# Weights' roundings queued behind evacuations, an earlier first memset, another queue for one load, and a new last quarter

## The chip, the cores and the metric

One core of one Trainium2 chip runs the kernel. The metric is the device time of one execution in microseconds (us), as the median of the timed runs. A profile is one further execution, recorded by the hardware profiler. TensorE (PE) multiplies matrices, VectorE (DVE), ScalarE (ACT) and GpSimd (POOL) work on tiles, and SyncE (SP) mostly issues DMAs. Each engine takes its own instructions strictly in order; between engines semaphores decide.

## The reference

One layer of an encoder for 2 x 256 tokens of width 1024, all in float32, with three branches on one normalized input:

```
h = rmsnorm(x);  proj = h @ w_in          # qkv | decays | z | cq | ckv | z_mla | q_mem | z_mem | gates
A: conv + silu on qkv, gated delta rule in both directions, rmsnorm per head, * silu(z)
B: q = rmsnorm(cq) @ w_q_up (+ rope), k|v = rmsnorm(ckv) @ w_kv_up (+ rope), softmax(q k) v, * silu(z_mla)
C: 4-head attention into 256 memory tokens, k|v = rmsnorm(mem) @ w_mem_kv, * silu(z_mem)
y = rmsnorm(x + (sum over branches of sigmoid(gate) * (o @ w_br)) @ w_out)
```

## The kernel before, in words

**Split products.** Every float32 operand is split into a high part (rounded to TensorE's fp32r) and a low part (the rest), and a product is three passes: high x high, low x high, high x low. Names end in h and l for data (`hh`, `hl`, `klh`, `kll`, `qlh`, `vh`, `vl`), and begin with `wh_` and `wl_` for weights. `weight()` (L224) brings a weight: SP loads it raw (`wr_`, L229), ACT rounds it to `wh_` (L241), DVE subtracts to get `wl_` (L244). Each of the three kinds has two buffers, so that a load waits for the subtraction two weights back and a rounding for the matmuls two weights back. `gemm` (L264) runs 24 matmuls of 512 columns for a weight of 1024 rows, 9 or 6 for a shorter one. `split()` (L249) evacuates a product from PSUM in the same two steps: ACT rounds (L252), DVE subtracts (L254).

**Stages.** The front (up to about 346 us) makes the memory keys and values (`mem_v`), the latents, and branch B: `mla_v` makes the values of four heads at a time (`v03`, `v10` to `v13`, first digit the half, second the token block), `mla_qk` the keys (`kn4`: head 4) and queries (`qn4`), `attend` the softmax and the product with the values (`a71`: head 7, half 1; `p_`, its transpose `pt_`, split to `ph_` and `pl_`, product `oa`). The rotary queries (`ra`, `rb`, then `rt`, split to `rh` and `rl`) go to DRAM (`d_q`) and come back in another layout (`qs`) by DMAs on SP. Tiles of branch A's projection (`qkv11`, `qkv18`, with a convolution on ACT and DVE: `cz`, `kq`, `vf`), z tiles (`za`) and gates (`g02`) fill the gaps. The middle runs branch A, the back the merge and `output`, which makes the rows of y in token blocks 0 to 3: the left half of all four, then the right half of blocks 0 to 2, then block 3's right half in two quarters, `y20` and `y21`.

**What sets the order.** The code issues steps, and a scheduler of the tile framework puts each engine's instructions into an order, by its own estimate of when they can run, by priority (`high_priority(offset=...)` puts an instruction ahead of others) and by explicit constraints: `issue_after(i)` keeps an instruction behind instruction i in the order, and adds no wait. In the middle, steps of branch A are generators with due times: `yield a, b` hands back the cost of a step and the distance after which the next is due.

**The places that the change touches.** In `mem_v` a 128x512 tile of zeros (`zero`, L387) feeds ten warm-up matmuls (`zp`, L390); `prm`, the small parameters (gains, convolution weights; 87 KB), is the second load on SP's queue (L405), and ACT and DVE need it for `mh`, the scaled memory tokens (L419, L420). In `attend` six matmuls (L366) run in the order (vh, ph), (vh, pl), (vl, ph) for each of two key blocks. In `gdn_out` the sum of squares of a head's output is reduced on DVE (L1181, into `rr`) and comes to TensorE a step later (`so`, L1185). In `output` the last quarter adds the residual on DVE (L1393), squares and sums (L1394), takes the power on GpSimd (L1396), and scales and stores.

Of the kernel before, what the change touches and what calls it, by code (L numbers as in the profile page):

```python
# [181 lines left out]
class Layer:  # L182
    def __init__(self, tc, A):
        self.tc, self.nc, self.A, self.hold = tc, tc.nc, A, None


# [37 lines left out]
    def weight(self, src, n, name, pool=None, into=None):  # L224
# [14 lines left out]
        hi = place("wh_", "wh")  # L239
        with self.tc.high_priority(offset=60):  # L240
            self.wround = nc.scalar.activation(hi[:, :n], raw[:, :n], AF.Copy).ins  # L241
# [78 lines left out]
    def attend(self, h, s, score, scale, vs, op, name):  # L320
# [40 lines left out]
        self.plast = self.lsplit  # L361
        n = 0
        for kb in range(2):
            q = slice(kb * 256, (kb + 1) * 256)
            for a, b in ((vs[kb][0], hi), (vs[kb][0], lo), (vs[kb][1], hi)):
                nc.tensor.matmul(pairs(op), a, turns(b[:, q]), start=n == 0, stop=n == 5)  # L366
# [12 lines left out]
    def mem_v(self):  # L379
        nc, A = self.nc, self.A  # L380
        ms = []
        warm = self.p0.tile([P, 1], F32, name="warm")
# [4 lines left out]
        nc.vector.memset(zero.bitcast(F32), 0.0)  # L387
        zp = self.ps_kk("zp")
        for i in range(10):
            nc.tensor.matmul(zp, zero[:, 0:P], zero, start=i == 0, stop=i == 9)  # L390

# [3 lines left out]
        with self.tc.high_priority(offset=1000):  # L395
            for k in range(8):
# [7 lines left out]
                if k == 0:  # L404
                    nc.sync.dma_start(self.prm, A["prm"])  # L405
# [740 lines left out]
    def gdn_out(self, hh):  # L1146
# [32 lines left out]
        with self.behind():  # L1179
            nc.vector.transpose(out=st, in_=sq)  # L1180
            nc.vector.tensor_reduce(red, st.rearrange("p (j i) -> p j i", i=32), axis=AX.X, op=ALU.add)  # L1181
# [140 lines left out]
    def output(self):  # L1322
# [16 lines left out]

        def product(ps, hi, lo, j, tb, c0=0, c1=512):  # L1340
            t = slice(tb * P, (tb + 1) * P)
            n = 0
            for q in range(2):
                for a, b in ((0, hi), (1, hi), (0, lo)):
                    nc.tensor.matmul(pairs(ps), xs[2 * j + q][a][:, t],  # L1345
                                     turns(b[:, q * 512:(q + 1) * 512])[:, c0 // 2:c1 // 2],
                                     start=j == 0 and n == 0, stop=j == 3 and n == 5)
# [34 lines left out]

        s3, out = ss[3], A["ys"][0, P:2 * P]
        for q in range(2):
            ps = self.ps_kk(f"y2{q}")
            for j in range(4):
                product(ps[:, 0:256], *ws[j], j, 3, 256 * q, 256 * q + 256)
            if q == 0:
                y = add(ps[:, 0:256], 3, 2, 256)
                nc.vector.tensor_scalar(s3[:, 0:1], s3[:, 1:2], 1.0 / D, s3[:, 0:1], ALU.mult, ALU.add)  # L1390
                nc.gpsimd.tensor_tensor(y, y, fg[:, 512:768], op=ALU.mult)
        y = ys[3][:, 768:1024]
        nc.vector.tensor_tensor(y, y, ps[:, 0:256], op=ALU.add)  # L1393
        nc.vector.tensor_tensor_reduce(self.ct("jk")[:, 0:256], y, y, 1.0 / D, s3[:, 0:1], ALU.mult, ALU.add, s3[:, 2:3])  # L1394
# [1 line left out]
        nc.gpsimd.tensor_tensor(r, s3[:, 2:3], self.c("hf")[:, 0:1], op=ALU.pow)  # L1396
# [1 line left out]
        nc.scalar.activation(ys[3][:, 0:448], ys[3][:, 0:448], AF.Copy, scale=r)
        nc.scalar.dma_start(out[:, 0:448], ys[3][:, 0:448])
        nc.vector.tensor_scalar(ys[3][:, 448:1024], ys[3][:, 448:1024], r, None, ALU.mult)  # L1400
# [321 lines left out]
```

## Time and profile before

| | |
|---|---|
| median of 3 runs | 798.67 us (798.55 to 798.84) |
| the profiled execution's own time | 798.48 us |
| its span | 796.7 us |
| TensorE busy | 786.6 us (99%) |
| VectorE busy | 579.2 us (73%) |
| ScalarE busy | 447.4 us (56%) |
| GpSimd busy | 166.9 us (21%) |
| granted TensorE clock | 0.999 |

How to read the rows. A row of the timeline is: start in us from the span's start, duration, engine and line, operation, tile written <- tiles read (without buffer numbers), shape, how many in a row, and in brackets how long the engine had been idle and what ended that. SPq and ACTq are DMA issues by these engines. A row of the waits names the engine and line that waited, what released it, and total, number and longest wait. A row of the DMA issues ends with the size of one and the median time from issue to landing. A matmul's duration includes its way through the array, so matmuls in a row start closer together than they last. TensorE's busy share is that of its queue being full, not of its peak.

### The profile page before, as it was taken

Reading aid. Unit: us, or ns where it says so; the run is one execution under the profiler, and the core shown is the slowest. Engines: PE = TensorE matmul, PEld = TensorE weight load, DVE = VectorE, ACT = ScalarE, POOL = GpSimd, SP = SyncE. Lnnn points to the kernel's source line nnn. Section 1 sums busy time; section 2 is a strip of 40 time slices with the busy share of each in tenths; the row PEclk is TensorE's granted clock in tenths of the full one; section 3 lists DMA queues with packets and bytes.
Section 4 is the critical chain, followed back from the end, with each engine's and each line's share of the span. In section 5 each row is a group of like instructions: output and inputs, shape, how many; then the busy total and the mean of one; then the engine's idle time right before and its main releaser. Section 6 shows DMA issues by size and latency. Waiting matters only on the chain.

```text
span 796.7 us, 13067 instructions
## 1 busy us (share of the span) xinstructions
PE 786.6 (99%) x4774; PEld 692.9 (87%) x4774; DVE 579.2 (73%) x974; ACT 447.4 (56%) x894; POOL 166.9 (21%) x135
## 2 busy tenths in 40 slices
PE   9999999999999999999999999999999999999996
PEld 7888898889898899988888888888888888888886
DVE  7886358787699999669599989498565655465543
ACT  6755465556565565646757556667766463322332
POOL 0200111000010002154221226540512003333312
PEclk9999999999999999999999999999999999999999
DMA  9523222732417635444444435555653557464532
GB/s 325 177 78 102 93 77 81 229 124 70 116 61 211 192 96 141 142 133 154 129 155 133 146 120 160 172 151 175 192 172 119 172 181 256 160 197 153 178 107 105
DMA packets 68911, 118.18 MB, mean 148 GB/s; under 512 B 23664, under 2 KB 31344, under 8 KB 68848
## 3 DMA queue, kind: packets, MB, share of 16 engines
q1 hardware_dynamic: 67552, 115.03, 45.9%
q10 hardware_dynamic: 1296, 2.33, 0.8%
q8 instruction: 37, 0.61, 0.3%
q14 instruction: 26, 0.21, 0.1%
HBM read 98.24 MB, written 19.09 MB: 147 GB/s over the span
## 4 chain that ended last, share of the span: by engine, by line
PE 91%; DVE 4%; DMA 1%; ACT 1%; issue 1%; POOL 0%; SPq 0%; POOLq 0%; ACTq 0%; DVEq 0%
PE gm_qkv L276 14%; PE gm_g L276 14%; PE gm_z L276 7%; PE gm_za L276 5%; PE gm_bm L276 5%; PE y L1345 5%; PE vm L427 3%; PE gm_be L276 3%; PE gm_qm L276 3%; PE gm_km L276 3%; PE gm_bg L276 3%; PE o L1163 2%; PE gm_bg L1312 2%; PE s_a L330 2%; PE kk L1012 2%; PE gm_qn L276 2%
## 5 line engine op out<-in xcount | busy, mean ns | idle before, releaser
L776 DVE SCALAR_TENSOR_TENSOR kq<-cz,prm,kq 128x510 f32<-128x510 f32 (+1 forms) x64 | 52.0, 813 | 2.2 <-ACT kq L769 1.3
L276 PE MATMUL gm_qkv<-hl,wh_qkv 128*128 128x512 f32 x192 | 49.0, 385 | 0.0
L276 PE MATMUL gm_g<-hh,wl_g 128*128 128x512 f32 x192 | 48.8, 384 | 0.0
L276 PE MATMUL gm_g<-hh,wh_g 128*128 128x512 f32 x192 | 48.0, 385 | 0.0
L276 PE MATMUL gm_g<-hl,wh_g 128*128 128x512 f32 x192 | 47.2, 382 | 0.0
L276 PE MATMUL gm_qkv<-hh,wl_qkv 128*128 128x512 f32 x192 | 47.0, 382 | 0.0
L276 PE MATMUL gm_qkv<-hh,wh_qkv 128*128 128x512 f32 x192 | 46.8, 381 | 0.0
L1287 POOL TENSOR_TENSOR mg<-mg,lg 128x512 f32<-128x512 f32 x16 | 29.5, 1849 | 73.2 <-DVE lg L1286 31.8
L244 DVE TENSOR_TENSOR wl_g<-wr_g,wh_g 128x1024 fp32r<-128x1024 f32 x24 | 31.2, 1300 | 17.1 <-PE gm_g L276 9.3
L244 DVE TENSOR_TENSOR wl_qkv<-wr_qkv,wh_qkv 128x1024 fp32r<-128x1024 f32 x24 | 31.0, 1290 | 13.6 <-ACT wh_qkv L241 7.7
L1022 DVE SCALAR_TENSOR_TENSOR ne<-e,cc,kk 128x512 f32<-128x512 f32 (+1 forms) x64 | 35.7, 608 | 6.2 <-ACT ed L843 2.7
L276 PEld LDWEIGHTS gm_qkv<-hh,wh_qkv 128*128 128x128 f32 x192 | 35.8, 189 | 5.1 <-ACT wh_qkv L241 0.3
L276 PEld LDWEIGHTS gm_g<-hl,wh_g 128*128 128x128 f32 x192 | 35.9, 189 | 4.7
L276 PEld LDWEIGHTS gm_qkv<-hh,wl_qkv 128*128 128x128 f32 x192 | 35.8, 189 | 4.8
L276 PEld LDWEIGHTS gm_g<-hh,wh_g 128*128 128x128 f32 x192 | 35.4, 189 | 4.8
L276 PEld LDWEIGHTS gm_qkv<-hl,wh_qkv 128*128 128x128 f32 x192 | 35.4, 189 | 4.7
L276 PEld LDWEIGHTS gm_g<-hh,wl_g 128*128 128x128 f32 x192 | 35.4, 189 | 4.5
L969 POOL TENSOR_SCALAR_AFFINE_SELECT e<-e 128x256 f32<-128x256 f32 x32 | 20.0, 651 | 90.2 <-DMA e<-d_r 75.1
L1345 PE MATMUL y<-wh_wo,mh 128*128 128x512 f32 (+1 forms) x144 | 37.7, 356 | 0.0
L241 ACT ACTIVATE wh_g<-wr_g 128x1024 fp32r<-128x1024 f32 x24 | 25.3, 1052 | 19.9 <-PE gm_g L276 7.2
L1188 POOL TENSOR_TENSOR rr<-rr,cst 32x16 f32<-32x16 f32 x8 | 25.0, 3123 | 46.6 <-DVE rr L1187 46.4
L241 ACT ACTIVATE wh_qkv<-wr_qkv 128x1024 fp32r<-128x1024 f32 x24 | 25.3, 1055 | 15.1 <-DVE vf L776 3.2
(458 smaller groups left out, 2189.4 us busy)
## 6 DMA issues: line engine op xcount, KB each, us to landing
wr_g<-in_w_dram SPq DMA_DIRECT2D x24, 512.0 KB, 4.0
wr_qkv<-in_w_dram SPq DMA_DIRECT2D x24, 512.0 KB, 3.8
e<-d_r SPq DMA_DIRECT2D x64, 96.0 KB, 3.0
wr_z<-in_w_dram SPq DMA_DIRECT2D x12, 512.0 KB, 3.6
d_g<-gt_g SPq DMA_DIRECT2D x16, 256.0 KB, 2.5
wr_za<-in_w_dram SPq DMA_DIRECT2D x8, 512.0 KB, 3.6
lg<-d_g SPq DMA_DIRECT2D x16, 256.0 KB, 3.9
wr_bm<-in_w_dram SPq DMA_DIRECT2D x8, 512.0 KB, 3.8
```

The lines of the kernel that those rows point to most:

```text
L241: self.wround = nc.scalar.activation(hi[:, :n], raw[:, :n], AF.Copy).ins
L244: self.wsplit = nc.vector.tensor_tensor(lo[:, :n], raw[:, :n], hi[:, :n].bitcast(F32), op=ALU.subtract).ins
L276: nc.tensor.matmul(pairs(ps[:m]), a[:, k * m:(k + 1) * m], turns(xs[k][j]), start=n == 0, stop=n == 3 * nk - 1)
L330: nc.tensor.matmul(pairs(sp[:, qb * 256:(qb + 1) * 256]), a, turns(b), start=j == 0, stop=j == n - 1)
L427: nc.tensor.matmul(pairs(vps[tb]), ms[k][a][:, t], turns(b[:, :512]), start=k == 0 and i == 0, stop=k == 7 and i == 2)
L776: nc.vector.scalar_tensor_tensor(ys, zs, self.cw[:, f, m:m + 1], ys, ALU.mult, ALU.add)
L969: self.nc.gpsimd.affine_select(out=e[:, :, r], in_=e[:, :, r], pattern=[[0, 2], [sg, 128]], compare_op=ALU.is_ge, fill=NEG, base=0, channe ...
L1012: nc.tensor.matmul(pairs(ps), a[:, k], turns(b), start=i == 0, stop=i == 2)
L1022: nev = nc.vector.scalar_tensor_tensor(ne[:, :, d, s, r], es[d][:, s, r].unsqueeze(1).to_broadcast([P, 2, n]), cc[:, d, w:w + 1], kin, ALU ...
L1188: nc.gpsimd.tensor_tensor(rr, rr, c("hf")[last, 0:1].to_broadcast([32, 16]), op=ALU.pow)
L1287: nc.gpsimd.tensor_tensor(self.merged[d], self.merged[d], gt, op=ALU.add)
L1345: nc.tensor.matmul(pairs(ps), xs[2 * j + q][a][:, t], turns(b[:, q * 512:(q + 1) * 512])[:, c0 // 2:c1 // 2], start=j == 0 and n == 0, sto ...
```

## The change

Five edits:

1. `free(a)` is new: `mla_v` and `mla_qk` register their evacuations in a bank, and `weight()` keeps its rounding and its subtraction behind the evacuations that were registered before the previous weight. It is an order on the same engine, not a wait.
2. `attend` for `a71` runs the four matmuls with `ph` ahead of the two with `pl`.
3. `mem_v` writes a 128x128 tile of zeros first (its matmuls read it four times over), and `prm` is loaded from GpSimd's queue.
4. `gdn_out` lets head 5's `so` come 13 instead of 12 later, as head 7's.
5. `output` puts the residual of the last quarter into PSUM (a first matmul that only opens the accumulation, then a copy over it), squares and sums on ACT from PSUM, and gives 480 columns of the last scaling to ACT and 544 to DVE, the last 256 of these straight from PSUM.

```diff
     def __init__(self, tc, A):
+        self.bank = [[], []]
...
-        with self.tc.high_priority(offset=60):
+        with self.tc.high_priority(offset=60), ExitStack() as st:
+            for i in self.bank[0]:
+                st.enter_context(self.tc.issue_after(i))
+            self.bank = [self.bank[1], []]
             self.wround = nc.scalar.activation(hi[:, :n], raw[:, :n], AF.Copy).ins
...
+    def free(self, a):
+        self.bank[1] += [a.ins, self.lsplit]
...
-        n = 0
-        for kb in range(2):
-            q = slice(kb * 256, (kb + 1) * 256)
-            for a, b in ((vs[kb][0], hi), (vs[kb][0], lo), (vs[kb][1], hi)):
-                nc.tensor.matmul(pairs(op), a, turns(b[:, q]), start=n == 0, stop=n == 5)
-                n += 1
+        order = [(kb, i, b) for kb in range(2) for i, b in ((0, hi), (0, lo), (1, hi))]
+        if name == "a71":
+            order.sort(key=lambda o: o[2] is lo)
+        for n, (kb, i, b) in enumerate(order):
+            nc.tensor.matmul(pairs(op), vs[kb][i], turns(b[:, kb * 256:(kb + 1) * 256]), start=n == 0, stop=n == 5)
...
+        zero = self.s2("zero", F32R)[:, 0:P]
+        nc.vector.memset(zero.bitcast(F32), 0.0)
         warm = self.p0.tile([P, 1], F32, name="warm")
...
-            nc.tensor.matmul(zp, zero[:, 0:P], zero, start=i == 0, stop=i == 9)
+            nc.tensor.matmul(zp, zero, zero.unsqueeze(1).to_broadcast([P, 4, P]), start=i == 0, stop=i == 9)
...
-                    nc.sync.dma_start(self.prm, A["prm"])
+                    nc.gpsimd.dma_start(self.prm, A["prm"])
...
-            self.split(ps, vh, vl)
+            self.free(self.split(ps, vh, vl))
...
-            self.split(unpaired(ps), halves(hi), halves(lo))
+            self.free(self.split(unpaired(ps), halves(hi), halves(lo)))
...
-        yield 0.0, 13 if hh == 7 else 12
+        yield 0.0, 13 if hh in (5, 7) else 12
...
+        parts = [self.ps_kk(f"y2{q}")[:, 0:256] for q in range(2)]
+        product(parts[1], *ws[0], 0, 3, 256, 512, 1)
+        nc.vector.tensor_copy(parts[1], y)
...
-        nc.vector.tensor_tensor(y, y, ps[:, 0:256], op=ALU.add)
-        nc.vector.tensor_tensor_reduce(self.ct("jk")[:, 0:256], y, y, 1.0 / D, s3[:, 0:1], ALU.mult, ALU.add, s3[:, 2:3])
+        nc.scalar.activation(self.ct("jk")[:, 0:256], ps, AF.Square, accum_out=s3[:, 2:3])
+        nc.vector.tensor_scalar(s3[:, 2:3], s3[:, 2:3], 1.0 / D, s3[:, 0:1], ALU.mult, ALU.add)
...
-        nc.vector.tensor_tensor(y, y, fg[:, 768:1024], op=ALU.mult)
-        nc.scalar.activation(ys[3][:, 0:448], ys[3][:, 0:448], AF.Copy, scale=r)
-        nc.scalar.dma_start(out[:, 0:448], ys[3][:, 0:448])
-        nc.vector.tensor_scalar(ys[3][:, 448:1024], ys[3][:, 448:1024], r, None, ALU.mult)
-        nc.sync.dma_start(out[:, 448:1024], ys[3][:, 448:1024])
+        nc.scalar.activation(ys[3][:, 0:480], ys[3][:, 0:480], AF.Copy, scale=r)
+        nc.scalar.dma_start(out[:, 0:480], ys[3][:, 0:480])
+        nc.vector.scalar_tensor_tensor(y, ps, r, fg[:, 768:1024], ALU.mult, ALU.mult)
+        nc.vector.tensor_scalar(ys[3][:, 480:768], ys[3][:, 480:768], r, None, ALU.mult)
+        nc.sync.dma_start(out[:, 480:1024], ys[3][:, 480:1024])
```

What the first edit does to the order shows on the engines' own lists. The numbers behind a name count buffers; the lines of the changed kernel are 4 to 7 higher. First ACT around the rounding of `qkv11`'s weight, before and after:

```order
L769 ACTIVATE kq2_1653<-cz_10_1654,prm_76 128x2x256
L241 ACTIVATE wh_qkv11_1703<-wr_qkv11_1701 128x1024
L252 ACTIVATE vh03_1681<-v03_1674 128x512
L241 ACTIVATE wh_qn0_1744<-wr_qn0_1742 128x384
L252 ACTIVATE kn0_1698<-gm_kn0_1691 128x512
```

```order
L774 ACTIVATE kq2_1653<-cz_10_1654,prm_76 128x2x256
L256 ACTIVATE vh03_1681<-v03_1674 128x512
L245 ACTIVATE wh_qkv11_1703<-wr_qkv11_1701 128x1024
L256 ACTIVATE kn0_1698<-gm_kn0_1691 128x512
L245 ACTIVATE wh_qn0_1744<-wr_qn0_1742 128x384
```

The two evacuations, `vh03` and `kn0`, have each changed places with the rounding ahead of them. The second place is ACT from `rh11` (rotary queries) to the rounding of `qn4`'s weight, before and after:

```order
L252 ACTIVATE rh11_2687<-rt_2682 128x512
L241 ACTIVATE wh_kn4_2886<-wr_kn4_2884 128x256
L767 ACTIVATE cz_18_2849<-gm_qkv18_2823 128x512
L769 ACTIVATE vf2_2848<-cz_18_2849,prm_76 128x512
L777 ACTIVATE cz_2_2776<-kq2_1653 128x512
L241 ACTIVATE wh_g03_2916<-wr_g03_2914 128x1024
L252 ACTIVATE vh11_2813<-v11_2806 128x512
L241 ACTIVATE wh_qn4_2954<-wr_qn4_2952 128x384
L252 ACTIVATE vh12_2869<-v12_2862 128x512
L252 ACTIVATE kn4_2901<-gm_kn4_2890 128x512
L252 ACTIVATE vh13_2880<-v13_2873 128x512
```

```order
L772 ACTIVATE cz_18_2849<-gm_qkv18_2823 128x512
L256 ACTIVATE rh11_2687<-rt_2682 128x512
L774 ACTIVATE vf2_2848<-cz_18_2849,prm_76 128x512
L782 ACTIVATE cz_2_2776<-kq2_1653 128x512
L256 ACTIVATE vh11_2813<-v11_2806 128x512
L245 ACTIVATE wh_kn4_2886<-wr_kn4_2884 128x256
L256 ACTIVATE vh12_2869<-v12_2862 128x512
L256 ACTIVATE vh13_2880<-v13_2873 128x512
L245 ACTIVATE wh_g03_2916<-wr_g03_2914 128x1024
L256 ACTIVATE kn4_2901<-gm_kn4_2890 128x512
L245 ACTIVATE wh_qn4_2954<-wr_qn4_2952 128x384
```

All four evacuations of the values and the keys now stand ahead of `wh_qn4`, three of them ahead of `wh_g03`, and `rh11` has come behind `cz_18`. On TensorE the same stretch, from the last value matmuls to the first with `g03`'s weight, before and after:

```order
L717 MATMUL v11_2806<-wl_wv1_2793,klh1_1113 128x512
L276 MATMUL gm_kn4_2890<-klh0_1108,wh_kn4_2886 128x512
L276 MATMUL gm_kn4_2890<-klh1_1113,wh_kn4_2886 128x512
L276 MATMUL gm_kn4_2890<-kll0_1109,wh_kn4_2886 128x512
L276 MATMUL gm_kn4_2890<-kll1_1114,wh_kn4_2886 128x512
L276 MATMUL gm_kn4_2890<-klh0_1108,wl_kn4_2888 128x512
L276 MATMUL gm_kn4_2890<-klh1_1113,wl_kn4_2888 128x512
L276 MATMUL gm_g03_2920<-hh0_339,wh_g03_2916 128x512
```

```order
L722 MATMUL v13_2873<-wl_wv1_2793,klh1_1113 128x512
L283 MATMUL gm_kn4_2890<-klh0_1108,wh_kn4_2886 128x512
L283 MATMUL gm_kn4_2890<-klh1_1113,wh_kn4_2886 128x512
L283 MATMUL gm_kn4_2890<-kll0_1109,wh_kn4_2886 128x512
L283 MATMUL gm_kn4_2890<-kll1_1114,wh_kn4_2886 128x512
L283 MATMUL gm_g03_2920<-hh0_339,wh_g03_2916 128x512
```

`v13` is now the last of the values instead of `v11`, and four instead of six `kn4` matmuls lie between it and `g03`; `gm_qkv18`'s end, which stood ahead of `v12` to `v11` (18 matmuls), now stands ahead of two of `v12`'s, `v11` and `v13` (14). The third place is TensorE ahead of `g02`, before and after:

```order
L276 MATMUL ra1_2625<-qlh2_897,wl_ra1_2630 128x512
L356 MATMUL pt_a21_2446<-cst_311,p_a21_2438 128x128 x4
L366 MATMUL oa2_2384<-ph_a20_2413,vh00_1607 128x256
L366 MATMUL oa2_2384<-pl_a20_2414,vh00_1607 128x256
L366 MATMUL oa2_2384<-ph_a20_2413,vl00_1608 128x256
L366 MATMUL oa2_2384<-ph_a20_2413,vh01_1618 128x256
L366 MATMUL oa2_2384<-pl_a20_2414,vh01_1618 128x256
L366 MATMUL oa2_2384<-ph_a20_2413,vl01_1619 128x256
L356 MATMUL pt_a30_2570<-cst_311,p_a30_2562 128x128 x4
L276 MATMUL gm_g02_2713<-hh0_339,wh_g02_2709 128x512
```

```order
L283 MATMUL ra1_2625<-qlh0_823,wl_ra1_2630 128x512
L283 MATMUL ra1_2625<-qlh1_859,wl_ra1_2630 128x512
L283 MATMUL ra1_2625<-qlh2_897,wl_ra1_2630 128x512
L846 MATMUL dp01_2078<-dr01ct_2055,bd_1325 128x512
L283 MATMUL gm_g02_2713<-hh0_339,wh_g02_2709 128x512
```

Before, the transposes of `a21` and `a30` and the products of `a20` stood between `ra1` and `g02`; now there is one matmul, `dp01`, and the attention's come later.

More of the change, by code (lines that the diff above doesn't have):

```diff
@@ L384, in mem_v @@
         nc.scalar.activation(warm, warm, AF.Square)
-        zero = self.s2("zero", F32R)
-        nc.vector.memset(zero.bitcast(F32), 0.0)
-        zp = self.ps_kk("zp")
+        zp = self.ps_kk("zp").rearrange("p (a b) -> p a b", a=4)
         for i in range(10):
-            nc.tensor.matmul(zp, zero[:, 0:P], zero, start=i == 0, stop=i == 9)
+            nc.tensor.matmul(zp, zero, zero.unsqueeze(1).to_broadcast([P, 4, P]), start=i == 0, stop=i == 9)
         vps = [self.ps_gm(f"vm{tb}") if tb == 3 else self.ps_ms(tb % 2, f"vm{tb}") for tb in range(4)]
@@ L1338, in output, with product @@
             ss.append(self.pe.tile([P, 4], F32, name=f"yss{tb}"))
-        def product(ps, hi, lo, j, tb, c0=0, c1=512):
+        def product(ps, hi, lo, j, tb, c0=0, c1=512, last=24, seeded=False):
             t = slice(tb * P, (tb + 1) * P)
@@ L1344, in product @@
                 for a, b in ((0, hi), (1, hi), (0, lo)):
-                    nc.tensor.matmul(pairs(ps), xs[2 * j + q][a][:, t],
-                                     turns(b[:, q * 512:(q + 1) * 512])[:, c0 // 2:c1 // 2],
-                                     start=j == 0 and n == 0, stop=j == 3 and n == 5)
+                    if 6 * j + n < last:
+                        nc.tensor.matmul(pairs(ps), xs[2 * j + q][a][:, t],
+                                         turns(b[:, q * 512:(q + 1) * 512])[:, c0 // 2:c1 // 2],
+                                         start=j == 0 and n == 0 and not seeded, stop=j == 3 and n == 5)
                     n += 1
@@ L1381, in output @@
             nc.sync.dma_start(out[:, 512:1024], y)
-        s3, out = ss[3], A["ys"][0, P:2 * P]
-        for q in range(2):
-            ps = self.ps_kk(f"y2{q}")
+        s3, out, y = ss[3], A["ys"][0, P:2 * P], ys[3][:, 768:1024]
+        parts = [self.ps_kk(f"y2{q}")[:, 0:256] for q in range(2)]
+        product(parts[1], *ws[0], 0, 3, 256, 512, 1)
+        nc.vector.tensor_copy(parts[1], y)
+        for q, ps in enumerate(parts):
             for j in range(4):
-                product(ps[:, 0:256], *ws[j], j, 3, 256 * q, 256 * q + 256)
+                product(ps, *ws[j], j, 3, 256 * q, 256 * q + 256, 24, q == 1)
             if q == 0:
-                y = add(ps[:, 0:256], 3, 2, 256)
+                x = add(ps, 3, 2, 256)
                 nc.vector.tensor_scalar(s3[:, 0:1], s3[:, 1:2], 1.0 / D, s3[:, 0:1], ALU.mult, ALU.add)
[L1391 to L1394, printed above, removed]
+                nc.gpsimd.tensor_tensor(x, x, fg[:, 512:768], op=ALU.mult)
+        nc.scalar.activation(self.ct("jk")[:, 0:256], ps, AF.Square, accum_out=s3[:, 2:3])
+        nc.vector.tensor_scalar(s3[:, 2:3], s3[:, 2:3], 1.0 / D, s3[:, 0:1], ALU.mult, ALU.add)
         r = self.pe.tile([P, 1], F32, tag="fr", bufs=4, name="fr3")
         nc.gpsimd.tensor_tensor(r, s3[:, 2:3], self.c("hf")[:, 0:1], op=ALU.pow)
-        nc.vector.tensor_tensor(y, y, fg[:, 768:1024], op=ALU.mult)
-        nc.scalar.activation(ys[3][:, 0:448], ys[3][:, 0:448], AF.Copy, scale=r)
-        nc.scalar.dma_start(out[:, 0:448], ys[3][:, 0:448])
-        nc.vector.tensor_scalar(ys[3][:, 448:1024], ys[3][:, 448:1024], r, None, ALU.mult)
-        nc.sync.dma_start(out[:, 448:1024], ys[3][:, 448:1024])
+        nc.scalar.activation(ys[3][:, 0:480], ys[3][:, 0:480], AF.Copy, scale=r)
[3 more added lines that the diff above has]
+        nc.sync.dma_start(out[:, 480:1024], ys[3][:, 480:1024])
     def run(self):
```

## The prediction

> **What bounds the kernel now.** I read the page first, then the chain of work that ended last, then what TensorE waits for.
>
> ```profile
> PE 91%; DVE 4%; DMA 1%; ACT 1%; issue 1%; POOL 0%; SPq 0%; POOLq 0%; ACTq 0%; DVEq 0%
> 728.18 20.72 PE gm_bg L276 x96
> ```
>
> The chain is TensorE from end to end (its second row: 96 matmuls of 512 columns in 20.72 us, 0.216 each, and half of that for 256 columns). So a microsecond counts only if TensorE stands still for it, or if it lies ahead of the first or behind the last matmul. TensorE's waits are few:
>
> ```profile
> PE gm_qn L276 <- DVE kn L254: 0.9, 1, 0.9
> PE oa L366 <- DVE pl_a L254: 0.3, 1, 0.3
> PE so L1185 <- DVE rr L1181: 0.3, 1, 0.3
> ```
>
> Each row is: who waits, for whom, total, times, longest. These three and the wait of the first matmul lie where the diff works; with the tail they are all that it can win. The sum is made against the profiled run's own 798.48 us (span 796.7); the median of the timed runs is 798.67, so 0.19 is added at the end. Anything under 0.2% (1.6 us) counts as no change, about what a measurement of this kernel can tell.
>
> **Start.** The zero tile shrinks to 128 columns and is written first; prm moves from SP's queue to GpSimd's.
>
> ```profile
> 1.18 0.42 SPq L405 DMA_DIRECT2D prm<-in_prm_dram  x1
> 1.49 4.63 PE L390 MATMUL zp<-zero 128*128 128x512 f32 x10 [1.49 <-DVE zero L387]
> 5.23 0.43 DVE L415 TENSOR_SCALAR wh_vm<-wr_vm 128x512 fp32r<-128x512 f32 x1 [2.52 <-DMA wr_vm<-in_wvm_dram]
> 5.53 0.91 ACT L419 ACTIVATE mh<-memT,prm 128x256 fp32r<-128x256 f32 x2 [2.84 <-DMA prm<-in_prm_dram]
> 5.69 0.69 DVE L422 TENSOR_TENSOR wl_vm<-wr_vm,wh_vm 128x512 fp32r<-128x512 f32 x1
> 6.09 0.87 PE L427 MATMUL vm<-wh_vm,mh 128*128 128x512 f32 x2
> 6.46 0.75 DVE L420 SCALAR_TENSOR_TENSOR mh<-memT,prm,mh 128x512 fp32r<-128x512 f32 x1
> memT<-in_memT_dram SPq DMA_DIRECT2D x3, 256.0 KB, 5.6
> ```
>
> zp can start about 0.4 earlier, but it is only warm-up. The first vm matmuls need mh (prm) and wh_vm (5.23 + 0.43 = 5.66), and the fifth needs mh's low half. VectorE makes that behind wl_vm, which ends at 6.38 whatever zp does; today it starts at 6.46. So of the 0.4 only some **0.1** gets through, if prm is no later than today. That is the open cost: no load on GpSimd's queue stands in this trace. The nearest rows are loads of SP: prm lands at about 5.5, 4.3 after its issue. On the new queue it can be issued at about 0.8, with no load ahead of it; with the 5.6 of the slowest early group (last row) it lands at 6.4, 0.9 late, and every bit of lateness moves mh and vm one for one. Bounds of the term: -0.1 to +0.9; I take -0.1, prm's own row being the nearest.
>
> A rule speaks against this move. The Trainium skill, SBUF — State Buffer, section "SBUF: two separate sides", says that GpSimd writes the descriptors of its DMAs itself and cannot while VectorE runs an operation that takes both its SBUF ports. VectorE's two memsets of ks lie just there; whether they take both ports no run here shows. The Trainium skill, DMA: Bandwidth & Descriptors, "Specifications", gives a first byte after about 1 us on this path against 0.6 on SP's; with that estimate prm would land where it lands now, and the start would give nothing.
>
> **The roundings behind the evacuations.** Nothing is added or removed; ACT and DVE get another order. Three places decide.
>
> (1) wh_qkv11. ACT runs without a pause and TensorE takes the weight when it is done:
>
> ```profile
> 158.48 0.73 ACT L769 ACTIVATE kq<-cz,prm 128x512 f32<-128x512 f32 x1
> 159.12 1.05 ACT L241 ACTIVATE wh_qkv<-wr_qkv 128x1024 fp32r<-128x1024 f32 x1
> 160.22 1.56 PE L276 MATMUL gm_qkv<-hh,wh_qkv 128*128 128x512 f32 x6
> ```
>
> 159.12 + 1.05 = 160.17 against 160.22: no slack. The order now puts vh03's evacuation ahead; such evacuations follow each other every 0.47 (268.80 and 269.27 below). **+0.45**, all of it on TensorE.
>
> (2) wh_g02 waits for ra1's high passes, since its buffer is theirs:
>
> ```profile
> 235.99 0.81 PE L276 MATMUL ra<-qlh,wl_ra 128*128 128x512 f32 x3
> 236.19 1.06 ACT L241 ACTIVATE wh_g<-wr_g 128x1024 fp32r<-128x1024 f32 x1 [1.18 <-PE ra L276]
> 238.10 1.11 PE L276 MATMUL gm_g<-hh,wh_g 128*128 128x512 f32 x4
> ```
>
> From the start of ra1's last pass (235.99) to the rounded weight are 1.26 us (236.19 + 1.06). Between them TensorE had 2.11 of work; in the new order only three ra1 matmuls and one of dp01 are left, 4 x 0.216 = 0.87. **+0.39**.
>
> (3) vh11 to wh_qn4.
>
> ```profile
> 254.04 0.63 ACT L252 ACTIVATE rh<-rt 128x512 fp32r<-128x512 f32 x1
> 255.83 0.42 SPq L695 DMA_DIRECT2D d_q<-rh  x1
> 259.61 0.60 ACT L767 ACTIVATE cz<-gm_qkv 128x512 f32<-128x512 f32 x1 [1.31 <-PE gm_qkv L276]
> 262.01 0.80 SPq L698 DMA_DIRECT2D qs<-d_q  x2
> 263.06 1.06 ACT L241 ACTIVATE wh_g<-wr_g 128x1024 fp32r<-128x1024 f32 x1 [1.58 <-PE v L717]
> 264.34 0.40 SPq L229 DMA_DIRECT2D wr_qn<-in_w_dram  x1
> 268.37 0.52 ACT L241 ACTIVATE wh_qn<-wr_qn 128x384 fp32r<-128x384 f32 x1 [3.76 <-DMA wr_qn<-in_w_dram]
> 268.80 0.58 ACT L252 ACTIVATE vh<-v 128x512 fp32r<-128x512 f32 x1
> 269.27 0.59 ACT L252 ACTIVATE kn<-gm_kn 128x512 fp32r<-128x512 f32 x1
> d_g<-gt_g SPq DMA_DIRECT2D x16, 256.0 KB, 2.5
> ```
>
> Now ACT waits 3.76 for wr_qn4's load with the evacuations vh12, kn4 and vh13 queued behind it, and gm_qn4 waits 0.91 for kn4. The new order puts them ahead: **-0.91**. What is late next is wh_g03, behind vh13. Between v13's last matmul and gm_g03 TensorE has four kn4 matmuls, 0.86; ACT needs one evacuation and one rounding, 0.5 + 1.06: at least 0.7. Counted from gm_qkv18's end, TensorE has 18 matmuls (3.89) while ACT has cz, rh11, vf2, cz, vh11, wh_kn4, vh12, vh13 and wh_g03, 0.63 + 0.5 + 0.63 + 0.5 + 3 x 0.47 + 0.4 + 1.06 = 5.1: 1.25. Between 0.7 and 1.3 I take **+0.9**.
>
> And rh11, today at 254.04 ahead of cz, comes behind it, to about 260.3. Its way to d_q and back to qs stands on SP ahead of wr_qn4. Today that way is long (d_q issued at 255.83, read back at 262.01, wr_qn issued at 264.34). With the 2.5 us of another 256 KB write (d_g, last row), wr_qn4 would be issued at about 266 and wh_qn4 be ready at about 270.4, against TensorE's need at 270.1: near 0.3. If the write took 6.2 as now, it would be some 2.5. Bounds 0 to 2.5; I take **+0.3**, as the queue is less full when that write starts.
>
> The three places: 0.45 + 0.39 - 0.91 + 0.9 + 0.3 = **+1.1**. The other weights up to 346 have more room in the trace than the order takes from them, and the small shifts in the first 60 us lie under matmuls that wait for nothing there; I put nothing for either. If that cover is gone, it is paid one for one, on the slower side.
>
> **a71.** The four matmuls that need only ph now stand ahead of the two that need pl:
>
> ```profile
> 346.38 0.69 DVE L254 TENSOR_TENSOR pl_a<-pt_a,ph_a 128x512 fp32r<-128x512 f32 x1 [3.89 <-ACT ph_a L252]
> 347.13 0.38 PE L366 MATMUL oa<-pl_a,vh 128*128 128x256 f32 x1 [0.35 <-DVE pl_a L254]
> ```
>
> Three more 256-column matmuls of 0.11 lie under pl: **-0.33**. ph is as close as before: four gm matmuls (0.86) now stand between the transposes and it.
>
> **so5** stands five gm matmuls (1.08) later, more than its wait: **-0.31**.
>
> **Tail.** One more matmul of 0.11 ahead of y20; then the sum of squares comes straight from PSUM on ACT:
>
> ```profile
> 788.87 0.42 ACT L1354 ACTIVATE jk<-y 128x256 f32<-128x256 f32 x1 [0.44 <-DVE y L1352]
> 789.19 0.19 ACT L1354 ACTIVATION_READ_ACCUMULATOR jk<-y 128x1 f32 x1
> 789.41 0.21 DVE L1390 TENSOR_SCALAR yss<-yss 128x1 f32<-128x1 f32 x1 [0.63 <-ACT jk L1354]
> 790.39 0.28 PE L1345 MATMUL y<-wl_wo,mh 128*128 128x256 f32 x1
> 790.70 0.42 DVE L1393 TENSOR_TENSOR y<-y,y 128x256 f32<-128x256 f32 x1 [1.07 <-PE y L1345]
> 791.73 0.79 POOL L1396 TENSOR_TENSOR fr<-yss,cst 128x1 f32<-128x1 f32 x1 [1.54 <-DVE yss L1394]
> 792.55 0.67 ACT L1398 ACTIVATE y<-y,fr 128x448 f32<-128x448 f32 x1 [3.17 <-POOL fr L1396]
> 792.55 0.52 DVE L1400 TENSOR_SCALAR y<-y,fr 128x576 f32<-128x576 f32 x1 [0.44 <-POOL fr L1396]
> 793.25 0.34 ACTq L1399 DMA_DIRECT2D out_dram<-y  x1
> ```
>
> ACT can start at 790.70 + 0.11 = 790.81, takes 0.51 with its accumulator, the small DVE step 0.21: the power starts at about 791.65 instead of 791.73, and without VectorE's multiplication beside it its 0.79 may shrink. Behind it ACT has 480 columns (0.72) and DVE 256 from PSUM and 288 more (0.42 + about 0.3) instead of 0.67 and 0.52; the later of the last two stores, 793.25 now, moves by -0.3 to +0.1. **-0.1**. The copy of the residual into PSUM lies beside y20's matmuls (2.6 us) and costs nothing.
>
> **Sum.** -0.1 + 1.1 - 0.33 - 0.31 - 0.1 = +0.25; 798.48 + 0.25 + 0.19 = **798.9**.
>
> **Rivals.**
> - The reorder pays (0.23). The wait at gm_qn goes and nothing takes its place, as ACT sat idle 1.58 and 3.76 between these very instructions, and could have begun wh_qkv11 and wh_g02 earlier if TensorE's order leaves more room. Then the term is -0.91 instead of +1.1: 798.9 - 2.0 = 796.9. Against it stands that vh13 must go ahead of wh_g03.
> - The order hardly matters (0.12): what one place wins the next gives back, and only the small edits stay: the term is 0: 797.8.
> - Slower: the rope's way through d_q holds wr_qn4 back (0.17). If its write takes 6.2 us as now and starts six later, gm_qn4 waits 2.5 and wh_g03 costs its 1.3: +2.6 on the forecast, 801.5. It decides once that write takes over 3 us, and exceeds 0.2% from about 4.
> - prm late on GpSimd's queue (0.08): +1.0 on the forecast, 799.9; slower by over 0.2% only from 0.5 beyond that bound.
>
> The forecast itself (0.4) spans 798.2 to 800.2. **How the numbers follow.** Faster by over 0.2% (under 797.07): the first rival, 0.23. Slower (over 800.27): the rope case, 0.17, and 0.05 of the forecast and of prm: 0.22. Within 0.2%: 0.55. The range leaves out the outer part of both sides: 796.8 to 801.5.
>
> **What would show it.** In the profile after: vm's first matmul at about 6.0, and what ACT's first mh waits for; a TensorE wait of about 0.4 at gm_qkv for wh_qkv near 160.6 and at gm_g near 237; one near 1 at gm_g for wh_g near 264 instead of gm_qn's 0.9; oa's wait under 0.1; none at so; the power at the end starting about 1.25 after the last matmul. It is wrong if TensorE shows no wait for a rounded weight (then the first rival), or if gm_qn waits over 1 for wh_qn (then the slower one).

## The result and the profile after

| | before | changed |
|---|---|---|
| median of 6 runs each | 798.61 us (798.43 to 799.14) | 803.83 us (802.38 to 806.05) |
| ratio, 95% interval | | 1.0067 [1.0052, 1.0082] |
| profiled execution | 798.48 us | 805.99 us |
| its span | 796.7 us | 804.1 us |

The change makes the kernel 5.2 us slower. The forecast of 798.9 and its range, which ended at 801.5, both missed. The profiled execution is one of the longest, so a second profile of the same kernel (803.99 us, experiment 6) is read beside it.

TensorE's waits after (who waits, for whom, total, times, longest):

```profile
PE gm_qkv L283 <- ACT wh_qkv L245: 1.5, 3, 0.6
PE vm L432 <- ACT mh L424: 1.5, 1, 1.5
PE gm_g L283 <- ACT wh_g L245: 1.1, 2, 0.8
PE zp L395 <- DVE warm L391: 1.1, 1, 1.1
PE gm_qn L283 <- ACT wh_qn L245: 0.8, 1, 0.8
PE gm_be L283 <- DVE zt_z L1229: 0.8, 1, 0.8
PE kk L1017 <- DVE ne L1027: 0.7, 1, 0.7
```

Before, there was no row for a rounded weight (`wh_`); now there are six such waits, 3.4 us together. The wait of `gm_qn` for `kn` is gone, as are those of `oa` and `so`. A second view says where the time is lost: how far each matmul starts behind the same matmul of before, where both orders have it.

```
TensorE behind before (us)       changed   repeat (exp. 6)
end of mem_v's first products      2.58      2.10
287 (gm_za, behind the front)      7.03      5.62
371                                6.60      5.19
end                                7.4       5.5
```

So 2.1 to 2.6 us are lost at the start, 3.5 to 4.5 in the front between 152 and 287, and little is won back behind it.

**The start.** The timeline from 1 us on, and under it TensorE's granted clock by stretches (stretch, its length, busy time and count of PE, PEld, DVE, ACT and POOL, clock, share of the DMA engines, GB/s). PEld is TensorE's loading of weights; a count takes in what only reaches into the stretch:

```profile
1.06 4.39 PE L395 MATMUL zp<-zero 128*128 128x512 f32 x10 [1.06 <-DVE warm L391]
1.25 0.75 POOL L410 DMA_DIRECT2D prm<-in_prm_dram  x1 [0.80 <-POOLq L1718]
6.42 0.91 ACT L424 ACTIVATE mh<-memT,prm 128x256 fp32r<-128x256 f32 x2 [3.73 <-DMA prm<-in_prm_dram]
6.98 3.02 PE L432 MATMUL vm<-wh_vm,mh 128*128 128x512 f32 x8 [1.53 <-ACT mh L424]
9.79 1.91 PE L432 MATMUL vm<-wl_vm,mh 128*128 128x512 f32 x4
...
5.03:8.45 3.42, 1.84 (x7) 0.91 (x6) 1.87 (x3) 2.03 (x5) 0.00 (x0) 1.00 0.99 375
8.45:11.86 3.41, 3.41 (x9) 2.71 (x9) 3.28 (x6) 3.41 (x8) 0.00 (x0) 0.50 1.05 390
11.86:15.27 3.41, 3.41 (x17) 2.97 (x16) 2.63 (x5) 2.60 (x5) 0.00 (x0) 1.00 1.06 399
```

`prm` lets ACT begin `mh` at 6.42 instead of 5.53. That was the feared end of the prediction's bounds. The warm-up begins and ends earlier, so TensorE stands still for 1.53 us. The ten matmuls of the warm-up ran at half clock (10 in 4.39 us, 0.43 each instead of 0.216). By the trace's record of the clock, full clock came at 5.03. Behind the stop it was lost again, from 8.45 to 11.86: 9 matmuls fall into that stretch, and 17 into the next one of the same length.

**The front.** ACT and TensorE at the places of the prediction:

```profile
162.19 1.04 ACT L245 ACTIVATE wh_qkv<-wr_qkv 128x1024 fp32r<-128x1024 f32 x1
163.29 1.99 PE L283 MATMUL gm_qkv<-hh,wh_qkv 128*128 128x512 f32 x8 [0.35 <-ACT wh_qkv L245]
171.30 1.99 PE L283 MATMUL gm_qkv<-hh,wh_qkv 128*128 128x512 f32 x8 [0.62 <-ACT wh_qkv L245]
239.66 0.70 PE L283 MATMUL gm_g<-hh,wh_g 128*128 128x512 f32 x2 [0.28 <-ACT wh_g L245]
268.82 1.07 ACT L245 ACTIVATE wh_g<-wr_g 128x1024 fp32r<-128x1024 f32 x1
269.95 1.99 PE L283 MATMUL gm_g<-hh,wh_g 128*128 128x512 f32 x8 [0.79 <-ACT wh_g L245]
277.00 0.92 PE L283 MATMUL gm_qn<-qlh,wh_qn 128*128 128x512 f32 x3 [0.83 <-ACT wh_qn L245]
```

The bracket at a row's end is shorter than the gap between matmuls, as the one before still drains. From start to start, less the usual 0.216, each wait is some 0.16 longer: 0.51 at `qkv11`, 0.78 at `qkv0`, 0.45 at `g02`, 0.95 at `g03`, 1.00 at `qn4`. To these come 0.74 at `qkv3` and 0.26 and 0.23 at `kn4`'s weight and `g03`'s low half, not quoted: 4.92 in all. The 1.07 that `gm_qn` used to wait for `kn` (0.91 by the profile) are gone, which leaves **+3.85** of the 4.45 lost in this stretch.

SP's list shows why `qn4`'s weight is late:

```profile
263.21 0.42 SPq L701 DMA_DIRECT2D d_q<-rl  x1
267.47 0.79 SPq L706 DMA_DIRECT2D qs<-d_q  x2
268.31 0.42 SPq L700 DMA_DIRECT2D d_q<-rh  x1
270.79 0.80 SPq L703 DMA_DIRECT2D qs<-d_q  x2
272.62 0.38 SPq L230 DMA_DIRECT2D wr_qn<-in_w_dram  x1
```

The write of `rl`, issued at 263.21, is back only at 267.4: the read `qs` waits for it in SP's queue, and behind it `rh11`'s write, its own read and then `wr_qn4`, issued 8.3 later than before (264.34).

**Tail.** After the last matmul (797.88):

```profile
798.70 0.21 DVE L1401 TENSOR_SCALAR yss<-yss 128x1 f32<-128x1 f32 x1 [1.69 <-ACT jk L1400]
798.99 0.55 POOL L1403 TENSOR_TENSOR fr<-yss,cst 128x1 f32<-128x1 f32 x1 [1.42 <-DVE yss L1401]
800.39 0.33 SPq L1408 DMA_DIRECT2D out_dram<-y  x1
```

The power starts 1.11 after that matmul (before 791.73 - 790.39 = 1.34) and takes 0.55 instead of 0.79; the last store is issued 2.51 after it instead of 2.86.

### The profile page after: what moved, and what is told of

Its sections match the earlier page's. It is cut to its first block, busy times and chain, and to the rows that moved or that the text cites. A ratio compares the mean times of both kernels' runs of the same rounds, so it can differ in the third digit from the quotient of the medians.

```text
span 804.1 us, 13056 instructions
## 1 busy us (share of the span) xinstructions
PE 789.9 (98%) x4775; PEld 693.6 (86%) x4775; DVE 578.4 (72%) x973; ACT 447.5 (56%) x896; POOL 169.4 (21%) x136
## 4 chain that ended last, share of the span: by engine, by line
PE 91%; DVE 4%; DMA 2%; ACT 1%; issue 1%; POOL 0%; POOLq 0%; ACTq 0%; DVEq 0%; SPq 0%
PE gm_g L283 15%; PE gm_qkv L283 14%; PE gm_z L283 8%; PE gm_za L283 5%; PE gm_bm L283 5%; PE y L1351 5%; PE vm L432 3%; PE gm_be L283 3%; PE o L1168 3%; PE gm_qm L283 3%; PE gm_km L283 3%; PE gm_bg L283 3%; PE kk L1017 2%; PE gm_bg L1317 2%; PE s_a L337 2%; PE gm_cq L283 2%
## 5 line engine op out<-in xcount | busy, mean ns | idle before, releaser
L781 DVE SCALAR_TENSOR_TENSOR kq<-cz,prm,kq 128x510 f32<-128x510 f32 (+1 forms) x64 | 49.4, 773 | 2.1 <-ACT kq L774 1.1
L248 DVE TENSOR_TENSOR wl_g<-wr_g,wh_g 128x1024 fp32r<-128x1024 f32 x24 | 33.1, 1380 | 16.9 <-PE gm_g L283 8.3
```

The lines of the kernel that those rows point to most:

```text
L781: nc.vector.scalar_tensor_tensor(ys, zs, self.cw[:, f, m:m + 1], ys, ALU.mult, ALU.add)
```

## The experiments

The theory: the reorder (edit 1) costs about 4 us, half of it at weights that the prediction gave no term; `prm`'s new queue costs the rest, by its lateness and by the clock. The rivals were: the loss is all in the front; the clock falls by chance; GpSimd's own way of issuing makes `prm` late; a single evacuation causes it all. Each ratio is against the kernel before on the same chip.

**1. Edit 1 alone**, put on the kernel before.

```diff
-            self.split(ps, vh, vl)
+            self.free(self.split(ps, vh, vl))
...
-            self.split(unpaired(ps), halves(hi), halves(lo))
+            self.free(self.split(unpaired(ps), halves(hi), halves(lo)))
```

> The kernel before with the first edit alone (the bank and free). Theory A (the reorder costs about what the new waits in the trace of after add up to, 4.9 us of waits for rounded weights between 160 and 280 less the 1.07 at gm_qn that it removes): 798.6 + 3.9 = 802.5. Rival B (those waits come mostly from the late start pushing TensorE and the loads out of step): within 1 us of before.

Measured 802.83 us against 798.78, 1.0050 [1.0036, 1.0063]: **+4.05**. TensorE is 0.24 late at 152 and 4.29 at 287, and the waits are those of the whole change:

```profile
PE gm_qn L283 <- ACT wh_qn L245: 1.1, 1, 1.1
PE gm_g L283 <- ACT wh_g L245: 1.1, 2, 0.8
PE gm_qkv L283 <- ACT wh_qkv L245: 0.9, 3, 0.3
```

The front's loss is edit 1's alone; it needs no late start.

**2. `prm` on GpSimd's queue alone.**

```diff
-                    nc.sync.dma_start(self.prm, A["prm"])
+                    nc.gpsimd.dma_start(self.prm, A["prm"])
```

> The kernel before with the load of prm alone moved to GpSimd's queue; the order on TensorE, ACT and DVE stays the same. Theory A (prm lands about 0.9 later, and the stop behind the warm-up lets TensorE's clock fall, so that vm runs its first ten or more matmuls at 427 instead of 216 ns): +1.5 to +2.6, that is 800.1 to 801.2, with runs further apart than before's 0.7. Rival B (the late landing alone): +0.9, 799.5.

Measured 799.89, 1.0013 [1.0004, 1.0022]: **+1.1**. `mh` starts at 6.32, 0.8 late:

```profile
6.32 0.91 ACT L419 ACTIVATE mh<-memT,prm 128x256 fp32r<-128x256 f32 x2 [3.64 <-DMA prm<-in_prm_dram]
6.88 2.32 PE L427 MATMUL vm<-wh_vm,mh 128*128 128x512 f32 x8 [0.76 <-ACT mh L419]
```

That is between the two forecasts. The lateness is there, but no loss of the clock: these eight matmuls take as long as before (2.32). The warm-up starts later here (1.49 as before) and leaves a stop of only 0.76. The 0.8 doesn't last, though: in this profile TensorE is 0.79 late at 152 and only 0.08 at 287, as the wait of `gm_qn` for `kn` (1.07 before) is gone, though edit 1 is not in this kernel. It ends 1.3 late by waits in the middle (`gm_be` 0.58, `gm_z`, `kk`). So that the +1.1 is the late load itself is not shown.

**3. The small edits alone**: `a71`'s order, `so5`, and the tail, as in the diff.

> The kernel before with a71's order, so5's place and the last quarter alone; start and roundings as before. By the sum of the prediction -0.33 - 0.31 - 0.1, about -0.75: 797.9. If the waits only move elsewhere: 798.6.

Measured 798.01, 0.9998 [0.9984, 1.0011]. By medians -0.77, about as expected, but not clear of the noise (one execution took 803.26). In its profile `a71`'s wait is 0.44 shorter, of which what follows up to 371 takes nearly all back (the lag is -0.75 at 345 and -0.77 at 371), and `so5`'s 0.47 is gone. It owes 0.57 to a place that these edits don't touch:

```profile
PE gm_qn L276 <- DVE kn L254: 0.3, 1, 0.3
```

Before, this wait was 0.9 by the same view; in the profiles that keep the order of before it runs from nothing (experiments 2 and 11) to 2.2 (experiment 13). The agreement with -0.75 is thus in part luck.

**4. The change with `prm` back on SP's queue.**

```diff
-                    nc.gpsimd.dma_start(self.prm, A["prm"])
+                    nc.sync.dma_start(self.prm, A["prm"])
```

> The changed kernel with prm back on SP's queue, its old place; TensorE, ACT and DVE keep the changed order. Theory A (prm's queue costs 1.5 to 2.6, the rest the front): 801.2 to 802.3, with runs no further apart than before's. Rival B (the front's reorder makes all of it): as the changed kernel, 803.8.

Measured 801.21, 1.0032 [1.0020, 1.0045]. `prm`'s queue is thus worth **2.6** of the 5.2 in the changed kernel, more than the 1.1 that it costs alone. `mem_v`'s first products are 0.07 early instead of 2.58 late; the front's waits stay (0.51, 0.34, 0.45, 0.95 and 1.13 at `qkv11`, `qkv0`, `g02`, `g03` and `qn4`).

**5. The change with 14 warm-up matmuls**, which cover the stop.

```diff
-        for i in range(10):
+        for i in range(14):
```

> The changed kernel with 14 instead of 10 warm-up matmuls, so that TensorE is busy until mh arrives; prm stays on GpSimd's queue, the order else stays but for a few squares of the memory tokens. Theory A (the stop of 1.5 us ahead of vm lets the clock fall for a stretch of vm in part of the executions, and this makes the changed kernel's spread): no matmul of vm at 427 ns behind the first two, all runs within 1 us near the changed kernel's fastest, 802.4. Rival B (the clock falls by a schedule of its own, or the spread has another source): as the changed kernel in the same call, 804 with runs 3 us apart.

Measured 802.63, 1.0054 [1.0040, 1.0068]: by medians 1.1 below the unaltered change beside it (next), but the two intervals overlap. No stop is left, and the clock is up from the first `vm` matmul on:

```profile
7.18 1.99 PE L432 MATMUL vm<-wh_vm,mh 128*128 128x512 f32 x8
```

The lag there is 0.77 instead of 2.10. The spread of the times (801.6 to 804.4) did not shrink as expected, so it isn't the clock's alone: in this profile `gm_z` waits 1.13 for `cz` in the middle, in others less or not at all.

**6. The change again**, beside experiment 5.

> The changed kernel again, on the chip of the run with 14 warm-up matmuls. Theory A: 802.3 to 806, in two groups about 1.9 apart by whether vm runs at 427 ns. Rival B: one group.

Measured 803.75, 1.0065 [1.0053, 1.0077]. The times fall in one group of 1.1 us, not in the two that were expected. The eight `vm` matmuls take 3.67, at 0.43 each:

```profile
6.83 3.67 PE L432 MATMUL vm<-wh_vm,mh 128*128 128x512 f32 x8 [1.14 <-ACT mh L424]
```

So did the ten of the warm-up (4.64 us). Here the clock didn't fall: it had not come up before the stop, and the trace records full clock at 10.27 only.

**7 and 8. Half of edit 1**: only the values' evacuations (`mla_v`), or only the keys' and queries' (`mla_qk`), go to the bank. Each has one of the two lines of experiment 1.

> The kernel before with the bank fed by the values' evacuations alone (mla_v), not by keys and queries. Theory A (each wait comes from the evacuation that its place in ACT's order names): the waits of 0.5 at wh_qkv11 (vh03 stays ahead) and of 0.95 at wh_g03 (vh13 stays ahead) remain, that of 0.3 to 0.8 at wh_qkv0 (kn0 and qnh0 back in place) goes; +2 to +3. Rival B (the reorder acts as a whole, through a late DVE): about as the first edit alone, +4.

> The kernel before with the bank fed by keys and queries alone (mla_qk). Theory A: no wait at wh_qkv11; wh_g03 has only vh11 ahead of it, so its wait of 0.95 goes; wh_qn4 stays behind the rope's way through d_q, 0.5 to 1.2 there; in all +0.5 to +1.5. Rival B: about as the first edit alone, +4.

The values alone: 802.59, 1.0050 [1.0037, 1.0063]; the keys and queries alone: 805.47, 1.0087 [1.0070, 1.0104]. Each half costs as much as the whole or more (+4.3 and +7.1), so the loss can't be shared out between them. With the values, `qkv11`'s 0.51 stays, but `g03`'s 0.95 goes, which wasn't expected; three waits of 0.3 to 0.5 appear that neither kernel has (`ss_x`, `s_a`, `ra`), and `qkv3` waits 0.78. With the keys and queries, `qkv11`, `qkv0` and `g03` don't wait, as expected, but `qkv3` waits 4.4, which nobody expected:

```profile
270.68 0.79 SPq L708 DMA_DIRECT2D qs<-d_q  x2
271.57 0.37 SPq L230 DMA_DIRECT2D wr_qkv<-in_w_dram  x1
276.01 1.06 ACT L245 ACTIVATE wh_qkv<-wr_qkv 128x1024 fp32r<-128x1024 f32 x1 [4.66 <-DMA wr_qkv<-in_w_dram]
277.12 3.66 PE L283 MATMUL gm_qkv<-hh,wh_qkv 128*128 128x512 f32 x8 [4.36 <-ACT wh_qkv L245]
...
277.00:281.00 4.00, 3.88 (x10) 3.10 (x11) 3.90 (x7) 1.38 (x4) 0.00 (x0) 0.57 0.34 123
```

The rope's way through DRAM holds the load of `qkv3`'s weight, and behind the stop TensorE again runs at half its clock (0.57 over 4 us, last row).

**9. Experiment 4's kernel without one link of the rope's way.**

```diff
-                nc.sync.dma_start(q1[o:o + 32], dq[0].rearrange("(h r) t -> r h t", h=4))
+                nc.sync.dma_start(q1[o:o + 32], self.d_q[g, 0 if g else j][0].rearrange("(h r) t -> r h t", h=4))
```

and the same for `q2`. The second part of the rotary queries is then a copy of the first, so this kernel leaves out a part of the computation.

> The changed kernel with prm on SP's queue, whose rotary queries of the second half are read back from d_q's first part, so that they no longer wait for rh11's and rl11's way through DRAM (this replaces part of the computation: the second part of those queries is a copy of the first). Orders on TensorE, ACT and DVE are the same. Theory A (that way holds wr_qn4 back on SP): wr_qn4 is issued 3 to 4 us earlier and the wait of 1.1 at wh_qn4 goes; but wr_qkv3 is still held by wl_g03 on DVE, so the wait at wh_qkv3 grows from 0.5 to 1 to 1.6, and the time falls by 0 to 0.6 against 801.2. Rival B (wr_qn4 waits for something else): the wait at wh_qn4 stays near 1.1.

Measured 801.32, 1.0047 [1.0029, 1.0064]. `wr_qn4` is issued at 268.24 instead of 269.85 (3 to 4 us earlier were expected), and `qn4`'s wait of 1.13 is gone. But `qkv3`'s grows from 0.49 to 0.84, and the time is that of experiment 4. The rope's way does hold `qn4`'s weight, but it isn't the only thing late there: `qkv3`'s load waits for DVE's subtraction of `g03`'s weight (2.9 on SP), which frees its buffer.

**10. Before with 6 warm-up matmuls**: a stop of 1.6 us ahead of `vm` without any late load.

```diff
-        for i in range(10):
+        for i in range(6):
```

> The kernel before with 6 instead of 10 warm-up matmuls; prm on SP's queue, in time. TensorE stands still for 2 us ahead of vm. Theory A (a stop ahead of vm leaves the clock low): 8 or more of vm's matmuls at 427 instead of 216, +1.3 to +2.5, though no load is late. Rival B (the low clock comes with the load on GpSimd's queue): vm at 216 from its second matmul, +0.

Measured 799.97, 1.0017 [1.0007, 1.0026].

```profile
6.02 3.78 PE L427 MATMUL vm<-wh_vm,mh 128*128 128x512 f32 x8 [1.61 <-ACT mh L419]
9.60 1.64 PE L427 MATMUL vm<-wl_vm,mh 128*128 128x512 f32 x4
```

`vm` starts on time, and its products end 1.97 late: that is the clock alone. The six of the warm-up run at half clock (0.43 each), and full clock comes at 10.83 instead of 6.46. The times run from 798.42 to 801.52, so it doesn't cost this in every execution; by medians it costs 1.15, less than the 1.3 to 2.5 expected.

**11 and 13. `prm` on ACT's queue**, with the small edits: second there, behind `wr_vm` (11), or first of all, ahead of it (13).

```diff
-                    nc.sync.dma_start(self.prm, A["prm"])
+                    nc.scalar.dma_start(self.prm, A["prm"])
```

In 13 this line also moves to the head of the loop over `k`, ahead of the first loads of `memT` and `wr_vm`.

> The kernel before with a71's order, so5's place and the last quarter, and prm as the second load on ACT's queue instead of SP's. Theory A (a queue of hardware loads costs prm nothing): prm lands by 5.5, 797.7 to 798.0. Rival B (any move off SP's second place makes prm late): +0.5 to +1 on that.

> The kernel before with a71's order, so5's place and the last quarter, and prm as the first load on ACT's queue, ahead of wr_vm. Theory A (the first loads land in the order of their issue over all queues, so prm is late only when the second memT load goes first): prm lands at about 5.0, with the first two loads; wr_vm, now behind it, by 5.5; no wait of 0.8 at vm; 797.7 to 798.2. Rival B (prm is late on every queue but SP's): prm at 6.2 again, 800.3.

Second on ACT's queue: 800.33, 1.0023 [1.0013, 1.0034]. First: 798.05, 0.9995 [0.9979, 1.0010]. The DMA issues (size, median from issue to landing), of 11, 13 and the changed kernel's twin, experiment 2:

```profile
prm<-in_prm_dram ACTq DMA_DIRECT2D x1, 87.0 KB, 5.1
...
prm<-in_prm_dram ACTq DMA_DIRECT2D x1, 87.0 KB, 4.0
...
prm<-in_prm_dram POOLq DMA_DIRECT2D x1, 87.0 KB, 5.1
```

Second on ACT's queue `prm` is as late as on GpSimd's. What makes it late is its place among all loads of the start, not the queue or the engine: in these traces the first loads land in the order of their issue. Before, `prm` was issued 0.47 ahead of the second load of `memT` and landed at 5.44, that load at 6.10. In experiments 2 and 11 that load is issued no later than `prm` and lands ahead of it (5.88 and 6.30, 6.08 and 6.28). When `prm` goes first, it lands at 4.74 (`mh` starts at 4.77), but then `wr_vm` lands at 5.91 instead of 5.21, and TensorE starts at 6.94 in that profile instead of 6.09.

**12 and 14. The small edits with the zero tile first**, without edit 1 and with `prm` on SP; 14 has 12 warm-up matmuls.

> The kernel before with a71's order, so5's place, the last quarter, and the zero tile of 128 columns first; prm on SP's queue, no bank. Theory A (an earlier warm-up only lengthens the stop ahead of vm): no gain over the small edits alone, 798.0, and in part of the executions the clock falls, up to +1.5. Rival B (the 0.4 gets through): 797.6.

> The small zero tile first, a71's order, so5's place and the last quarter, prm on SP's queue, no bank, and 12 warm-up matmuls that reach up to vm. Theory A (with no stop ahead of vm the clock does not fall): vm at 216 from its second matmul on, 797.5 to 797.9, runs no further apart than before's. Rival B: as with 10 warm-up matmuls, 797.7 with a few runs 1.5 to 2 above.

Measured 797.72, 0.9992 [0.9983, 1.0000], and 798.48, 0.9998 [0.9989, 1.0006]. The first is the best version found, some 1 us below before by medians, with an interval that just reaches no change. The zero tile gives nothing in that profile: `vm` starts at 5.80 instead of 6.09, with its first three matmuls at half clock, and ends 0.06 late. Twelve warm-up matmuls don't reach up to `vm` in 14's profile, where full clock came early (4.34): a stop of 0.68 is left. Its 798.48 is above the 797.5 to 797.9 expected.

## Why the prediction failed, step by step

**What held.** Where the prediction gave a place its own row, the size was right: `qkv11` 0.51 (forecast 0.45), `g02` 0.45 (0.39), `g03` 0.95 (0.9), `gm_qn`'s wait for `kn` gone (1.07 against 0.91). These four come to +0.84; forecast was +0.83. `a71` won 0.44 (0.33), which the changed kernel keeps up to 371, and `so5` 0.47 (0.31), and the last store 0.35 (0.1) behind the last matmul, of which about 0.1 is seen at the span's end.

**The term that failed first: "The other weights up to 346 have more room in the trace than the order takes from them ... I put nothing".** They wait 2.0 in the profile after (`qkv0` 0.78, `qkv3` 0.74, 0.26, 0.23). `qkv0` had 0.95 of room before: its rounding ended at 166.49, its first matmul came at 167.44. Its load (row of issue, row of the rounding that takes it), before and then after:

```profile
161.95 0.35 SPq L229 DMA_DIRECT2D wr_qkv<-in_w_dram  x1
165.43 1.06 ACT L241 ACTIVATE wh_qkv<-wr_qkv 128x1024 fp32r<-128x1024 f32 x1 [2.94 <-DMA wr_qkv<-in_w_dram]
...
165.02 0.35 SPq L230 DMA_DIRECT2D wr_qkv<-in_w_dram  x1
170.19 1.06 ACT L245 ACTIVATE wh_qkv<-wr_qkv 128x1024 fp32r<-128x1024 f32 x1 [2.10 <-DMA wr_qkv<-in_w_dram]
```

The issue moved by 3.07, just as TensorE's lag there (2.58 + 0.51), so by the order alone the room would have held. But the load now takes 5.17 instead of 3.48: 1.69 more, less 0.95 of room, is 0.74, about the wait. It isn't chance: in all six profiles with the whole of edit 1 it takes 4.5 to 5.2 (after and experiments 1, 4, 5, 6, 9), in the eight with the order of before 3.5 to 3.6. Why the same load is slower there stays open. `qkv3` had 1.05 of room. Its load stands on SP behind the rope's way, as in experiment 8, but the last that it waited for in the profile after was its buffer, which DVE's subtraction of `g03`'s weight frees:

```profile
SPq L230 <- DVE wl_g L248: 1.1, 1, 1.1
```

The lesson is the same at both: room was counted on the engine that rounds, and what used it up was a load that came later or took longer.

**The rope, "I take +0.3, as the queue is less full when that write starts".** `qn4` waits 1.00 after, and 0.7 to 1.7 in experiments 1, 4, 5 and 6. The mechanism was named, with bounds of 0 to 2.5 that hold, but it was sized by a write of 2.5 us on a free queue. The first half's write of `rl` took 4.2, and `rh11`'s own write stands behind it. Experiment 9 shows that shortening this way only hands the wait on to `qkv3`. The need of 270.1 in the prediction stands there without its working; the rows give 270.84 - 0.91 = 269.93.

**The start, "I take -0.1, prm's own row being the nearest".** It was the other end of the bounds, +0.9, that came true (6.42 against 5.53), and the larger part of the loss, the clock, had no term at all. The rows hold what was overlooked: the warm-up's ten matmuls take 4.63 us, 0.43 each, so it runs at half clock up to its end; a warm-up that ends earlier and an `mh` that comes later make one stop; and what stands behind it was priced at full clock. Experiments 5 and 10 separate the two: without the stop the lag is 0.77, with a stop and no late load it is 1.97. By the medians of the changed kernel and experiment 4 the start costs 2.6.

The Trainium skill, DMA: Bandwidth & Descriptors, section "Issuing engines are not separate DMA queues", says that DMAs from all engines run on the same 16 DMA engines and interleave. Experiments 11 and 13 agree (5.1 as second on another queue, 4.0 as first). The rule weighed in the prediction, on GpSimd's descriptors and VectorE, isn't needed for it. The Trainium skill, TensorE: Matmul & The Clock Gate, section "What's actually happening", gives half clock by default and after an idle window of about 3.4 us, in windows that run free of the kernel. The length agrees: the slow stretches of the profile after and of experiments 8 and 11 last 3.41. But no whole window was idle in the profile after: a stop of 1.53 us after full speed was enough.

**The sum by medians.** Apart, edit 1 gives +4.05 (experiment 1), `prm`'s queue +1.1 (2) and the small edits -0.8 (3): 4.4 of the 5.2. Together, the queue costs 2.6, 1.5 more than alone. Two things in the profiles go that way: the early warm-up makes the stop longer (1.53 and 1.14 against 0.76), and half clock behind it makes 2.1 to 2.6 at the start out of about 0.8; and alone, the lateness was taken up at `gm_qn`'s wait for `kn`, which edit 1 has removed. How much is each one's, no run shows. The rest of the change costs 2.4 (experiment 4), 0.9 less than its parts apart (3.3). In the profiles `a71`'s 0.44 lasts in experiment 4 (the lag goes from 3.84 at 345 to 3.39 at 371) and hardly in experiment 3. Where the rest is won stays open; waits of the middle that differ by up to 1 us from run to run (`gm_be`, `gm_z`) could hide it, which is argued and not shown.

**The chances.** The slower side had 0.22, from two rivals that were thought of one at a time. Both came together, the rope in part (1.00 of the 2.5 at `qn4`) and the late `prm` in full (0.9), beside a front that lost where no rival looked and a clock that none named.

## What to carry to other kernels

An order that "adds no wait" on its engine still moves every release behind it, of buffers, loads and writes on a queue: count the room of each later consumer from the load's issue on, not from the engine that rounds, and ask for the room left when the load is a microsecond slower. When a load at the start is moved, write down all first loads in order of issue over all queues; here its place in this list, not its queue, said when it lands. And where an edit lengthens a stop of TensorE near the start, price what follows at half clock, too.
